# Tree attention on one core: the Q and K of 40 more heads laid side by side by GpSimd before TensorE turns them, and two groups of output rows stored in other pieces

## Chip, cores and metric

One core of a Trainium2 chip. The time is device microseconds (us) of one execution; the kernel before took 133.55 us (median of three runs, 133.35 to 133.63).

## What is computed

The reference, cut to what matters: attention over 512 tokens that are the nodes of a binary tree (parent of i is (i-1)//2), where a node sees itself and its ancestors only. There are 8 x 12 = 96 heads of dimension 64, float32 in and out.

```python
scores = np.einsum('bhqd,bhkd->bhqk', Q, K) * scale
scores = scores + (1 - mask) * (-1e9)        # mask[i, j] = 1 for j = i and its ancestors
weights = np.exp(scores - np.max(scores, axis=-1, keepdims=True))
weights = weights / (np.sum(weights, axis=-1, keepdims=True) + 1e-10)
return np.einsum('bhqk,bhkd->bhqd', weights, V).astype(np.float32)
```

## The kernel before

**Units of work.** The 96 heads go in 48 pairs. Pair i (from 8 on, the "wide" pairs) goes through these steps. *Turn* (L456 for K, L483 for Q; one call serves two pairs): TensorE transposes Q and K with an identity into the PSUM tiles `ktp` and `qtp`, and VectorE copies these to a tile `kq` (L470, L474, L478 for K, L493 for Q). *Scores* (L507, L536): TensorE adds products of mask codes and of keys with queries into PSUM, for the 128 top nodes (`s1`) and for the lower ones (`s2`); ScalarE takes the exponential (L529, L560) into bf16 tiles. *Values* (L592): 20 products per head pair of these weights with V and a column of ones, into the PSUM tile `ob`, of which there is one. *Norm* (L644): VectorE takes the reciprocal of the ones' column (L651) and multiplies (L653) into the output tile `of`.

**Loads.** Q, K and V are float32 in DRAM and become bf16 on the way: all loads but the first two are DMAs issued by GpSimd (POOL in the profile). Q and K come in blocks of 8 heads (tiles `qst`, `kst`, four of each), V in groups of 16 heads (`vst`, three). V isn't used as it lies: copies ("spreads", all on L364) bring its rows to other partitions in the `vt` tiles, of which there are two sets. VectorE makes some of these copies (a table by pair), ScalarE a few early ones, GpSimd the rest.

**Laying.** A block's Q or K can be turned in two ways. `turn_slot` (L437) transposes each head of a pair by itself: 16 transposes of 128 x 64 per call. For a block in `LAID` (8, 9, 10 and 11, so heads 64 to 95), GpSimd first copies the block into `beside["K"]` or `beside["Q"]` so that the two heads of a pair stand side by side (`lay`, L426: two copies of 128 x 512 words for a block, each for four heads), and a call has 8 transposes of 128 x 128 (L441). There is one `beside` tile for K and one for Q, so that a block can be laid only when the block laid before it has been turned.

**The order of values.** `values` does the full-width products first and the ones of half width (64 columns) last; from pair 4*LAID[0]-4 = 28 on the half-width ones stand in the middle (L630).

**GpSimd's order.** GpSimd works through a list written out by hand (`pool_program`, L676): DMA issues, spreads, lays and stores, strictly one after the other; an entry's wait holds back all behind it. DMAs are told of by eight semaphores in turn, so that a DMA also waits for the landing of the one eight before it. The outputs are stored by GpSimd too (L662), but for the last four heads, which SyncE stores at the very end. The first four heads go in four DMAs of 85, 2, 34 and 7 of the 128 partitions (`DEALT`, L669), between loads; all other stores take all partitions.

Of the kernel before, what the change touches and what calls it, by code (L numbers as in the profile page):

```python
# [119 lines left out]
def kernel(  # L120
# [7 lines left out]
    nc = tc.nc  # L128
    B, H, S, D = Q.shape
    P = nc.NUM_PARTITIONS  # L130
# [5 lines left out]
    WIDE = 8  # L136
    KB, VB, VO = 8, 16, 16
    EIGHT = 2
    LAID = (8, 9, 10, 11)
    assert NH % VB == 0  # L140

    fp32 = mybir.dt.float32
# [90 lines left out]
    issued = {(name, h) for name in ("kst", "qst") for h in (0, 1)}  # L233
# [35 lines left out]
    def head(i, a):  # L269

        return 2 * i + a if i < WIDE else 4 * (i // 2) + i % 2 + 2 * a
# [151 lines left out]
    def slots(st, i):  # L423
        return st[2 * i // KB].rearrange("p (g x) t d -> p g (x t) d", x=2)

    def lay(name, b):  # L426

        st = {"kst": ksts, "qst": qsts}[name][b]
        assert all((name, h) in issued for h in range(KB * b, KB * b + KB))
        laid[name, b] = two = beside[name[0].upper()]  # L430
        for g in range(KB // 4):
            src = st[:, 4 * g:4 * g + 4, :, :].rearrange("p (a x) t d -> p (x t) a d", x=2)
            nc.gpsimd.tensor_copy(
                out=two[:, g, :, :, :].bitcast(int32), in_=src.bitcast(int32)
            )
# [156 lines left out]
    def values(i):  # L592

        if i < NP - 1:
            obs[i] = ob = psO.tile([P, 2, 512], fp32, name="ob")
        else:
            obs[i] = ob = psS.tile([P, 2, 512], fp32, name="s1")
        e1, e2, vt = ets[i], e2s[i % NE], vts[(head(i, 0) // VB) % NV]

        vtile = VTILE if i < WIDE else WVTILE  # L600
        parts = EIGHT_PARTS if head(i, 0) >= VB * EIGHT else PARTS[i >= WIDE]
        assert all(("vt", n, head(i, a)) in issued for n in parts for a in range(2))

        def product(e, a, t, tile_v, lo=0, hi=128, **flags):
            nc.tensor.matmul(  # L605
                out=ob[lo:hi, a, 65 * t:65 * t + 65],
                lhsT=e[:, a, PLACE[t], lo:hi],
                rhs=vt[vtile[tile_v][0]][:, head(i, a) % VB, vtile[tile_v][1], 0:D + 1],
                **flags,
            )  # L610

        def firsts(a):
            for t in range(4):
                product(e1, a, t, 0, start=t == 0, stop=False)

        def halves(a, last=True):
            for t in (0, 1):
                product(e2, a, t, 1 + SELF[t], 0, 64, start=False, stop=last and t == 1)
                product(e2, a, t, 1 + t, 64, 128, start=False, stop=last and t == 1)

        def wholes(a, last=False):
            for t in (2, 3):
# [37 lines left out]
    def store(eng, h0, n, step=1, p0=0, p1=P):  # L660
        g, f = divmod(h0, VO)
        return eng.dma_start(  # L662
            out=Or[p0:p1, h0:h0 + step * (n - 1) + 1:step, :],
            in_=ofs[g][p0:p1, f:f + step * (n - 1) + 1:step, :, :].rearrange(
                "p h t d -> p h (t d)"
            ),
        )

    DEALT = (0, 85, 87, 121, P)  # L669

    def store_rows(j0, j1):

        for j in range(j0, j1):
            store(nc.gpsimd, 0, 4, 1, DEALT[j], DEALT[j + 1])

    def pool_program():  # L676

        ops = [
            (load_k, 2, 2), (load_q, 2, 2), (load_v, 0, 4), (load_v, 4, 4),
            (load_k, 4, 4), (load_q, 4, 4), (load_k, 8, 4),  # L680
            (load_q, 8, 4), (load_v, 8, 8), (load_k, 12, 4),
            (load_q, 12, 4), (load_k, 16, 8), (load_q, 16, 4), (load_rows, 1, "upper"),
            (load_rows, 1, "even"), (load_rows, 1, "odd"), (load_q, 20, 4),
            (load_k, 24, 8), (load_q, 24, 8), (load_rows, 2, "upper"),
            (load_k, 32, 8), (load_leaves, 2, 0), (load_leaves, 2, 1),
            (load_q, 32, 8), (load_rows, 3, "upper"),
            (spread_pool, (1, "Z0", 8, 16), (1, "Z1", 8, 16)),
            (load_k, 40, 8), (load_q, 40, 8), (load_leaves, 3, 0), (load_leaves, 3, 1),
            (spread_top, 2, 0, 16), (spread_pool, (2, "Z0", 0, 16), (2, "Z1", 0, 16)),
            (load_q, 48, 8), (spread_pool, (2, "X", 0, 16)),  # L690
            (load_k, 48, 8), (spread_pool, (2, "N", 0, 16)),
            (load_rows, 4, "upper"), (spread_top, 3, 0, 16),
            (load_k, 56, 8), (load_q, 56, 8), (load_leaves, 4, 0), (load_leaves, 4, 1),
            (spread_pool, (3, "X", 0, 16), (3, "N", 0, 16), (3, "Z0", 0, 16), (3, "Z1", 0, 16)),
            (load_k, 64, 8), (store_rows, 0, 2), (load_q, 64, 8), (store_rows, 2, 4),
            (load_k, 72, 8), (spread_top, 4), (store, nc.gpsimd, 4, 12), (lay, "kst", 8),
            (load_q, 72, 8), (spread_pool, (4, "X", 0, 16), (4, "N", 0, 16)),
            (lay, "qst", 8), (load_rows, 5, "upper"),
            (spread_pool, (4, "Z0", 0, 16), (4, "Z1", 0, 16)),
            (load_leaves, 5, 0), (load_leaves, 5, 1), (load_k, 80, 8), (load_q, 80, 8),  # L700
            (store, nc.gpsimd, 16, 8), (lay, "kst", 9), (load_k, 88, 8), (load_q, 88, 8),
            (lay, "qst", 9), (store, nc.gpsimd, 24, 8), (store, nc.gpsimd, 32, 16),
            (spread_top, 5), (lay, "kst", 10), (store, nc.gpsimd, 48, 16), (lay, "qst", 10),
            (spread_pool, (5, "X", 0, 16), (5, "N", 0, 16)),
            (spread_pool, (5, "Z0", 0, 16), (5, "Z1", 0, 16)),
            (lay, "kst", 11), (store, nc.gpsimd, 64, 8), (lay, "qst", 11),
            (store, nc.gpsimd, 72, 8), (spread_leaves, 5, 1),
            (store, nc.gpsimd, 80, 8), (store, nc.gpsimd, 88, 4),
        ]
        return ops  # L710
# [146 lines left out]
```

## Time and profile before

| | |
|---|---|
| median of 3 runs | 133.55 us |
| the profiled execution: its time, its span | 133.8 us, 131.9 us |
| busy in the span: PE, DVE, ACT, POOL | 114.7, 108.8, 94.4, 87.1 us |
| granted TensorE clock, mean | 0.978 |
| HBM read and written | 37.96 MB, 12.58 MB |

How to read it: PE is TensorE, DVE VectorE, ACT ScalarE, POOL GpSimd, SP SyncE. Times in the rows are us from the span's start. A row of the timeline has the start, the duration, engine, line, operation, output <- input, shape and count, and in brackets the idle time just before it with what ended it. A row of a group has the busy sum and the mean in ns. DMA share is the time of the packets as a share of 16 DMA engines; it passes 1 where packets overlap.

### The profile page before, as it was taken

Reading aid. Unit: us, or ns where it says so; the run is one execution under the profiler, and the core shown is the slowest. Engines: PE = TensorE matmul, PEld = TensorE weight load, DVE = VectorE, ACT = ScalarE, POOL = GpSimd, SP = SyncE. Lnnn points to the kernel's source line nnn. Section 1 sums busy time; section 2 is a strip of 40 time slices with the busy share of each in tenths; the row PEclk is TensorE's granted clock in tenths of the full one; section 3 lists DMA queues with packets and bytes.
Section 4 is the critical chain, followed back from the end, with each engine's and each line's share of the span. In section 5 each row is a group of like instructions: output and inputs, shape, how many; then the busy total and the mean of one; then the engine's idle time right before and its main releaser. Section 6 shows DMA issues by size and latency. Waiting matters only on the chain.

```text
span 131.9 us, 5281 instructions
## 1 busy us (share of the span) xinstructions
PE 114.7 (87%) x2286; PEld 80.4 (61%) x2289; DVE 108.8 (82%) x261; ACT 94.4 (72%) x153; POOL 87.1 (66%) x118
## 2 busy tenths in 40 slices
PE   6883999999789699899899999999988999999920
PEld 2351576676566476666577677677765766776610
DVE  3438569988999989989999999999999999877350
ACT  4358268989768957968858787787868668688900
POOL 6994624245623998799951899999999977802200
PEclk9999599999999999999999999999999999999996
DMA  3999999999999999999999999999999999999984
GB/s 122 216 190 196 198 199 205 199 199 207 206 200 205 204 202 208 209 202 205 202 208 204 244 236 305 338 204 207 203 288 285 228 391 406 400 402 402 397 315 148
DMA packets 29719, 32.28 MB, mean 245 GB/s; under 512 B 1488, under 2 KB 26704, under 8 KB 29696
## 3 DMA queue, kind: packets, MB, share of 16 engines
q0 software_dynamic: 28416, 30.68, 115.2%
q1 hardware_dynamic: 864, 0.93, 2.1%
q10 hardware_dynamic: 416, 0.33, 1.0%
q8 instruction: 18, 0.29, 0.8%
q14 instruction: 5, 0.04, 0.1%
HBM read 37.96 MB, written 12.58 MB: 383 GB/s over the span
## 4 chain that ended last, share of the span: by engine, by line
DVE 38%; PE 24%; DMA 14%; POOL 10%; issue 5%; ACT 3%; ACTq 1%; POOLq 0%
DVE of L653 12%; DVE vt L364 11%; DMA kst<-in_K_dram 8%; PE ob L605 8%; DMA qst<-in_Q_dram 6%; POOL vt L364 5%; DVE rec L651 3%; PE s L511 3%; DVE kq L493 3%; DVE kq L470 3%; DVE kq L478 3%; DVE kq L474 3%; PE s L519 2%; ACT e L560 2%; PE s L544 1%
## 5 line engine op out<-in xcount | busy, mean ns | idle before, releaser
L529 ACT ACTIVATE e<-s 128x1024 bf16<-128x1024 f32 x40 | 40.9, 1023 | 20.7 <-PE s L519 20.1
L605 PE MATMUL ob<-vt,e 128*128 128x65 bf16 (+1 forms) x940 | 39.8, 198 | 6.0 <-DVE of L653 3.0
L605 PEld LDWEIGHTS <-e 128*128 128x128 bf16 (+1 forms) x960 | 31.7, 103 | 15.9 <-DVE of L653 5.1
L560 ACT ACTIVATE e<-s 128x384 bf16<-128x384 f32 x80 | 34.7, 491 | 0.0
L653 DVE TENSOR_TENSOR of<-ob,rec 128x512 f32<-128x512 f32 x47 | 32.5, 691 | 1.6
L364 POOL COPY vt<-vst 32x512 int32<-32x512 int32 (+1 forms) x38 | 31.0, 816 | 2.9 <-PE ob L605 1.2
L364 DVE COPY vt<-vst 32x1024 bf16<-32x1024 bf16 (+6 forms) x54 | 26.8, 497 | 2.3 <-DMA vst<-in_V_dram 1.3
L662 POOL DMA_DIRECT2D out_dram<-of x13 | 12.1, 928 | 12.7 <-DVE of L653 9.2
L511 PE MATMUL s<-codes 40*128 40x512 bf16 x96 | 19.3, 398 | 0.7 <-ACT e L525 0.4
L519 PE MATMUL s<-kq 64*128 64x512 bf16 x96 | 18.5, 380 | 0.0
L651 DVE RECIPROCAL rec<-ob 128x8 f32<-128x8 f32 x47 | 9.6, 204 | 8.8 <-PE ob L605 8.0
L554 PEld LDWEIGHTS <-kq 64*128 64x128 bf16 x320 | 12.1, 94 | 4.8
L554 PE MATMUL s<-kq 64*128 64x160 bf16 (+1 forms) x320 | 14.6, 208 | 0.0
L544 PE MATMUL s<-codes 40*128 40x384 bf16 x80 | 13.6, 333 | 0.3
L493 DVE COPY kq<-qtp 128x1024 bf16<-128x1024 bf16 x20 | 13.6, 681 | 0.0
L256 POOL DMA_DIRECT2D qst<-in_Q_dram x11 | 8.3, 752 | 6.8 <-DMA vst<-in_V_dram 2.6
L525 ACT ACTIVATE e<-s 128x1024 bf16<-128x1024 f32 x8 | 8.2, 1022 | 6.0 <-PE s L519 5.9
L544 PEld LDWEIGHTS <-codes 40*128 40x128 bf16 x80 | 6.1, 94 | 7.9 <-issue 1.2
L256 POOL DMA_DIRECT2D kst<-in_K_dram x10 | 7.6, 760 | 3.9 <-PE ob L605 2.8
L470 DVE COPY kq<-ktp 128x256 bf16<-128x256 bf16 x20 | 8.3, 415 | 0.3 <-PE ktp L450 0.3
L474 DVE COPY kq<-ktp 128x256 bf16<-128x256 bf16 x20 | 8.3, 415 | 0.0
L478 DVE COPY kq<-ktp 128x512 bf16<-128x512 bf16 x20 | 8.3, 414 | 0.0
(49 smaller groups left out, 139.4 us busy)
## 6 DMA issues: line engine op xcount, KB each, us to landing
kst<-in_K_dram POOLq DMA_DIRECT2D x10, 512.0 KB, 13.2
out_dram<-of POOLq DMA_DIRECT2D x5, 1024.0 KB, 13.9
qst<-in_Q_dram POOLq DMA_DIRECT2D x9, 512.0 KB, 14.5
out_dram<-of POOLq DMA_DIRECT2D x2, 2048.0 KB, 20.8
vst<-in_V_dram POOLq DMA_DIRECT2D x12, 256.0 KB, 14.9
vst<-in_V_dram POOLq DMA_DIRECT2D x6, 512.0 KB, 14.3
out_dram<-of POOLq DMA_DIRECT2D x1, 1536.0 KB, 10.7
qst<-in_Q_dram POOLq DMA_DIRECT2D x5, 256.0 KB, 11.9
```

The source lines that it names most:

```text
L256: return nc.gpsimd.dma_start(out=kept[b][:, h0 % KB:h0 % KB + n, :, :].rearrange("p (g x) t d -> p g (x t d)", x=2), in_=wide[:, h0 // 2:( ...
L364: return copy(out=dst, in_=src)
L493: nc.vector.tensor_copy(out=qq[:, :, 0:16, :].rearrange("p b u c -> p b (u c)"), in_=halves)
L511: nc.tensor.matmul(out=sp[:, a, :], lhsT=(k1code if i < WIDE else k1wide)[64 * a:64 * a + CODE_ROWS, :], rhs=(q1code[64 * a:64 * a + CODE_ ...
L519: nc.tensor.matmul(out=sp[:, a, :], lhsT=keys(i, a, TOP), rhs=qTs[i][64 * a:64 * a + 64, :, :].rearrange("p t c -> p (t c)"), start=False, ...
L529: ) if i < WIDE else nc.scalar.activation(
L544: nc.tensor.matmul(out=flat[:, a, :, :].rearrange("p u (t c) -> p u t c", t=4)[:, :, :, 16:64], lhsT=k2wide[64 * a:64 * a + CODE_ROWS, :], ...
L554: nc.tensor.matmul(out=flat[:, a, :, lo:hi], lhsT=keys(i, a, WTILE2[t]), rhs=qT[64 * a:64 * a + 64, :, lo:hi], start=False, stop=t == 1, s ...
L560: nc.scalar.activation(out=e2s[i % NE][:, a, :, 32:128].rearrange("p t (r u) -> p t r u", u=2), in_=flat[:, a, :, :].rearrange("p u (t r) ...
L605: nc.tensor.matmul(out=ob[lo:hi, a, 65 * t:65 * t + 65], lhsT=e[:, a, PLACE[t], lo:hi], rhs=vt[vtile[tile_v][0]][:, head(i, a) % VB, vtile ...
L651: nc.vector.reciprocal(out=rec[:, a:a + n, :, :], in_=o4[:, a:a + n, :, D:D + 1])
L653: nc.vector.tensor_tensor(out=ofs[g][:, first:last + 1:step, :, :], in0=o4[:, a:a + n, :, 0:D], in1=rec[:, a:a + n, :, :].to_broadcast([P, ...
```

## The change

Three things are changed. (1) `LAID` becomes blocks 2, 3, 4, 5, 7 to 11: heads 16 to 47 and 56 to 63 are laid too, and `lay` can do one half of a block. The pair from which the order of values differs stays 28. (2) The dealt stores have three heads (0 to 2) and not four; the store after them takes heads 3 to 15. (3) Heads 32 to 34 leave the store of heads 32 to 47 and go in three DMAs of 15, 17 and 96 partitions, later in the list, among the lays of blocks 10 and 11. To make room some entries of the list change places: `spread_top` of V's group 3 goes behind the loads of heads 56 to 63.

```diff
-    LAID = (8, 9, 10, 11)
+    LAID = (2, 3, 4, 5, 7, 8, 9, 10, 11)
+    LATE = 28
...
-    def lay(name, b):
+    def lay(name, b, g0=0, g1=2):
...
-        for g in range(KB // 4):
+        for g in range(g0, g1):
...
-        elif i >= 4 * LAID[0] - 4:
+        elif i >= LATE:
...
-            store(nc.gpsimd, 0, 4, 1, DEALT[j], DEALT[j + 1])
+            store(nc.gpsimd, 0, 3, 1, DEALT[j], DEALT[j + 1])
...
-            (load_k, 24, 8), (load_q, 24, 8), (load_rows, 2, "upper"),
-            (load_k, 32, 8), (load_leaves, 2, 0), (load_leaves, 2, 1),
-            (load_q, 32, 8), (load_rows, 3, "upper"),
+            (load_k, 24, 8), (load_q, 24, 8), (load_rows, 2, "upper"), (lay, "kst", 2),
+            (load_k, 32, 8), (lay, "qst", 2, 0, 1), (load_leaves, 2, 0), (load_leaves, 2, 1),
+            (load_q, 32, 8), (lay, "qst", 2, 1, 2), (load_rows, 3, "upper"),
...
-            (lay, "qst", 9), (store, nc.gpsimd, 24, 8), (store, nc.gpsimd, 32, 16),
-            (spread_top, 5), (lay, "kst", 10), (store, nc.gpsimd, 48, 16), (lay, "qst", 10),
+            (lay, "qst", 9), (store, nc.gpsimd, 24, 8), (store, nc.gpsimd, 35, 13),
+            (spread_top, 5), (lay, "kst", 10), (store, nc.gpsimd, 32, 3, 1, 0, 15),
+            (store, nc.gpsimd, 48, 16), (lay, "qst", 10), (store, nc.gpsimd, 32, 3, 1, 15, 32),
...
-            (lay, "kst", 11), (store, nc.gpsimd, 64, 8), (lay, "qst", 11),
+            (lay, "kst", 11), (store, nc.gpsimd, 32, 3, 1, 32, P), (store, nc.gpsimd, 64, 8), (lay, "qst", 11),
```

GpSimd's rows from the loads of V's group 3 (heads 48 to 63; `vst` in the first row) to the last spread of group 2 (heads 32 to 47; `vt` 107 to 109) stand like this before the change; the load of `qst` is that of heads 48 to 55:

```order
L294 DMA vst<-in_V_dram 32x8x512 x2
L364 COPY vt_0_107<-vst 32x16x32 x4
L364 COPY vt_1_108<-vst 32x32x32 x2
L256 DMA qst<-in_Q_dram 128x4x512
L364 COPY vt_2_109<-vst 32x32x32
```

And so after it:

```order
L295 DMA vst<-in_V_dram 32x8x512 x2
L434 COPY besideK<-kst 128x512 x2
L365 COPY vt_0_107<-vst 32x16x32 x4
L365 COPY vt_1_108<-vst 32x32x32 x2
L257 DMA qst<-in_Q_dram 128x4x512
L434 COPY besideQ<-qst 128x512 x2
L365 COPY vt_2_109<-vst 32x32x32
```

Block 4's keys (heads 32 to 39) are laid ahead of six spreads, and its queries behind them and a load's issue.

TensorE's rows where it turns the queries of the first heads of block 4, behind the last products of values (`ob`, half width), before:

```order
L605 LDWEIGHTS e_1_103
L605 MATMUL ob<-vt_1_114,e_1_103 64x65
L450 LDWEIGHTS qst
L450 MATMUL qtp<-ptile,qst 64x2x64
L450 LDWEIGHTS qst
L450 MATMUL qtp<-ptile,qst 64x2x64
```

The same place after:

```order
L606 LDWEIGHTS e_1_103
L606 MATMUL ob<-vt_1_114,e_1_103 64x65
L442 LDWEIGHTS besideQ
L442 MATMUL qtp<-ptile,besideQ 128x2x64
L442 LDWEIGHTS besideQ
L442 MATMUL qtp<-ptile,besideQ 128x2x64
```

Before, 16 such transposes read the loaded tile; now 8 of double width read GpSimd's copy of it, and stand behind GpSimd's wait. TensorE's program has 4260 rows, 320 fewer than the 4580 of before; VectorE's and ScalarE's rows are the same in number and order.

More of the change, by code (lines that the diff above doesn't have):

```diff
@@ L424, in slots @@
         return st[2 * i // KB].rearrange("p (g x) t d -> p g (x t) d", x=2)
-    def lay(name, b):
+    def lay(name, b, g0=0, g1=2):
         st = {"kst": ksts, "qst": qsts}[name][b]
-        assert all((name, h) in issued for h in range(KB * b, KB * b + KB))
+        assert all((name, h) in issued for h in range(KB * b + 4 * g0, KB * b + 4 * g1))
         laid[name, b] = two = beside[name[0].upper()]
-        for g in range(KB // 4):
+        for g in range(g0, g1):
             src = st[:, 4 * g:4 * g + 4, :, :].rearrange("p (a x) t d -> p (x t) a d", x=2)
@@ L683, in pool_program @@
             (load_rows, 1, "even"), (load_rows, 1, "odd"), (load_q, 20, 4),
[L684 to L688 removed]
+            (load_k, 24, 8), (load_q, 24, 8), (load_rows, 2, "upper"), (lay, "kst", 2),
+            (load_k, 32, 8), (lay, "qst", 2, 0, 1), (load_leaves, 2, 0), (load_leaves, 2, 1),
+            (load_q, 32, 8), (lay, "qst", 2, 1, 2), (load_rows, 3, "upper"),
+            (spread_pool, (1, "Z0", 8, 16), (1, "Z1", 8, 16)), (lay, "kst", 3),
+            (load_k, 40, 8), (load_q, 40, 8), (lay, "qst", 3),
+            (load_leaves, 3, 0), (load_leaves, 3, 1), (lay, "kst", 4),
             (spread_top, 2, 0, 16), (spread_pool, (2, "Z0", 0, 16), (2, "Z1", 0, 16)),
[L690 removed]
+            (load_q, 48, 8), (lay, "qst", 4), (spread_pool, (2, "X", 0, 16)),
             (load_k, 48, 8), (spread_pool, (2, "N", 0, 16)),
[L692 to L693 removed]
+            (load_rows, 4, "upper"), (lay, "kst", 5),
+            (load_k, 56, 8), (load_q, 56, 8), (lay, "qst", 5),
+            (load_leaves, 4, 0), (load_leaves, 4, 1), (spread_top, 3, 0, 16),
             (spread_pool, (3, "X", 0, 16), (3, "N", 0, 16), (3, "Z0", 0, 16), (3, "Z1", 0, 16)),
[L695 to L696 removed]
+            (load_k, 64, 8), (store_rows, 0, 2), (load_q, 64, 8), (store_rows, 2, 3),
+            (lay, "kst", 7), (store_rows, 3, 4),
+            (load_k, 72, 8), (lay, "qst", 7), (spread_top, 4), (store, nc.gpsimd, 3, 13), (lay, "kst", 8),
             (load_q, 72, 8), (spread_pool, (4, "X", 0, 16), (4, "N", 0, 16)),
```

## Prediction

> **What bounds the kernel now.** I read the page's 40 slices first (busy tenths, 3.3 us each), then the stages, then the rows of single waits. The DMA engines are full from the second slice to the 38th, GpSimd from the 23rd to the 34th:
>
> ```profile
> POOL 6994624245623998799951899999999977802200
> DMA  3999999999999999999999999999999999999984
> ```
>
> The stages show what sets the pace (us; then busy time and count of PE, PEld, DVE, ACT, POOL; granted clock, DMA share, GB/s):
>
> ```profile
> 60.00:65.00 5.00, 4.65 (x115) 3.34 (x110) 4.82 (x12) 4.18 (x7) 4.86 (x6) 1.00 1.36 203
> 65.00:70.00 5.00, 4.66 (x112) 3.42 (x109) 4.84 (x12) 3.57 (x7) 2.80 (x4) 1.00 1.24 206
> 90.00:95.00 5.00, 4.84 (x99) 3.58 (x98) 4.84 (x12) 3.96 (x8) 5.00 (x8) 1.00 1.26 205
> ```
>
> In the middle VectorE works 4.8 of 5 us, the rest being gaps of some hundredths between instructions: the chain of pairs runs at VectorE's pace. GpSimd has room (2.80 of 5) at 65 to 70 and none at 90 to 95. The DMA queue never empties, but loads are asked for some 13 us before they land, so it doesn't hold the pairs up. What ends the program is the last pair's norm and SyncE's store behind it:
>
> ```profile
> 126.96 0.42 DVE L653 TENSOR_TENSOR of<-s,rec 128x256 f32<-128x256 f32 x1
> 127.41 0.39 SPq L662 DMA_DIRECT2D out_dram<-of  x1
> out_dram<-of POOLq DMA_DIRECT2D x1, 512.0 KB, 5.3
> out_dram<-of SPq DMA_DIRECT2D x1, 512.0 KB, 3.6
> 124.42 0.76 POOL L662 DMA_DIRECT2D out_dram<-of  x1 [3.42 <-DVE of L653]
> 127.00:128.00 1.00, 0.00 (x0) 0.00 (x0) 0.39 (x1) 0.00 (x0) 0.00 (x0) 1.00 0.57 217
> ```
>
> SyncE's store lands at 127.41 + 3.6 = 131.0, GpSimd's last at 124.42 + 5.3 = 129.7. The DMA share drops to 0.57 at 127 to 128: most DMA engines have run dry and wait for that store, while the last one still writes GpSimd's rows until 129.7. So a later norm moves the end, but for the part that hides behind the last DMA engine.
>
> **The laid transposes give TensorE nothing.** Both forms are in the trace:
>
> ```profile
> 71.68 0.79 PE L605 MATMUL ob<-vt,e 128*128 128x65 bf16 x20
> 72.30 0.61 PE L450 MATMUL qtp<-ptile,qst 128*64 128x128 bf16 x16
> 72.85 0.40 PE L511 MATMUL s<-codes 40*128 40x512 bf16 x2
> 83.04 0.89 PE L605 MATMUL ob<-vt,e 128*128 128x65 bf16 x20
> 83.77 0.61 PE L441 MATMUL ktp<-ptile,besideK 128*128 128x128 bf16 x8
> 84.31 0.40 PE L511 MATMUL s<-codes 40*128 40x512 bf16 x2
> ```
>
> Sixteen narrow transposes take 0.55 us to the next row (72.30 to 72.85), eight wide ones 0.54. Twenty calls change form, worth 20 x 0.01 = 0.2 us. Against it stands that full width follows half width at once: values take 0.62 us to the next row in the old order and 0.73 in the one that changes width twice, so up to 20 x 0.11 = 2.2 us more of TensorE. I take 0 of both, for TensorE waits for VectorE's norm there (row at 50.85 below); ends -0.2 and +2.2.
>
> **What GpSimd's 20 more copies cost VectorE.** Five blocks, Q and K, two copies each:
>
> ```profile
> L433 POOL COPY besideQ<-qst 128x512 int32<-128x512 int32 x8 | 5.3, 680 | 0.2
> L433 POOL COPY besideK<-kst 128x512 int32<-128x512 int32 x8 | 4.7, 612 | 1.1 <-PE ktp L441 0.9
> L364 POOL COPY vt<-vst 32x1024 int32<-32x1024 int32 x16 | 17.3, 1078 | 0.7
> L364 POOL COPY vt<-vst 32x512 int32<-32x512 int32 x22 | 13.8, 626 | 2.2 <-PE ob L605 1.2
> L364 DVE COPY vt<-vst 32x1024 bf16<-32x1024 bf16 x36 | 19.6, 543 | 1.9 <-DMA vst<-in_V_dram 1.3
> 70.16 0.42 DVE L364 COPY vt<-vst 32x1024 bf16<-32x1024 bf16 x1
> 99.84 1.05 DVE L364 COPY vt<-vst 32x1024 bf16<-32x1024 bf16 x1
> ```
>
> 10 x 0.68 + 10 x 0.61 = 12.9 us. VectorE's own spreads take 0.42 us when GpSimd rests (70.16) and up to 1.05 beside its work (99.84). Their mean of 0.543 makes 36 x 0.12 = 4.4 us lost to 5.3 + 4.7 + 17.3 + 13.8 = 41.1 us of GpSimd's copying, 0.11 us per us. The new 12.9 us cost 1.4 by this; 0 if none meets a spread, 12.9 x 0.11 x 2 = 2.8 if they meet twice as many.
>
> **Where TensorE will wait for GpSimd.** I add GpSimd's rows up in the new order. The load that stands ahead of the first piece waits for a landing in both kernels:
>
> ```profile
> 42.41 0.58 POOL L294 DMA_DIRECT2D vst<-in_V_dram  x1 [1.92 <-DMA kst<-in_K_dram]
> 43.03 4.86 POOL L364 COPY vt<-vst 32x512 int32<-32x512 int32 x6
> 47.84 0.76 POOL L256 DMA_DIRECT2D qst<-in_Q_dram  x1
> 48.64 1.03 POOL L364 COPY vt<-vst 32x1024 int32<-32x1024 int32 x1
> 77.44 1.20 POOL L433 COPY besideK<-kst 128x512 int32<-128x512 int32 x2
> 49.01 0.61 PE L450 MATMUL qtp<-ptile,qst 128*64 128x128 bf16 x16
> 50.85 0.79 PE L605 MATMUL ob<-vt,e 128*128 128x65 bf16 x20 [0.28 <-DVE of L653]
> ```
>
> From 43.03: block 4's keys 1.2 (44.23), six spreads 4.81 (49.04), the load's issue 0.80 (49.84), the first half of block 4's queries 0.68: 50.52. TensorE wants them at 49.01, so it waits 1.5 us; behind it stand the scores of the next pair and its values, for which VectorE's norm waits. From the turn to these values are 50.85 - 0.28 - 49.01 = 1.56 us of work, so the values start at 52.08 and not 50.85: **1.2 us**, on VectorE's path. Copies slowed before 49 us make TensorE come later to the same point, so they are covered by this wait; the ends of this term are 0 (GpSimd is earlier, or the pairs are 1.2 us late by themselves) and 1.5. Behind it the lays of blocks 5 and 7, eight copies, 5.2 us, cost 5.2 x 0.11 = **0.6 us** by the rate above. The other lays come in time by the same sum.
>
> ```profile
> 57.57 1.17 POOL L294 DMA_DIRECT2D vst<-in_V_dram  x2
> 63.37 0.77 POOL L256 DMA_DIRECT2D kst<-in_K_dram  x1
> 68.10 1.08 POOL L662 DMA_DIRECT2D out_dram<-of  x1 [1.38 <-DMA kst<-in_K_dram]
> 71.28 0.56 POOL L662 DMA_DIRECT2D out_dram<-of  x1 [2.10 <-DMA qst<-in_Q_dram]
> 72.89 0.78 POOL L256 DMA_DIRECT2D kst<-in_K_dram  x1 [1.04 <-PE ob L605]
> kst<-in_K_dram POOLq DMA_DIRECT2D x10, 512.0 KB, 13.2
> ```
>
> With `spread_top` of group 3 moved down, the load of 63.37 is issued at about 67.7. What was issued at 57.57 to 58.7 lands some 13 us later, at 71 to 72, so the queue doesn't run dry there, by 3 us. GpSimd's idle 1.38 + 2.10 + 1.04 = 4.5 us before 72.89 take the delay in but for some 1.5 us.
>
> **The stores.** Three DMAs more (15, 17 and 96 rows); bytes stay.
>
> ```profile
> out_dram<-of POOLq DMA_DIRECT2D x1, 340.0 KB, 13.8
> out_dram<-of POOLq DMA_DIRECT2D x1, 8.0 KB, 12.9
> q8 instruction: 18, 0.29, 0.8%
> ```
>
> The 8 KB store (2 rows) was issued 1.12 us behind that of 340 KB and landed 0.2 behind it: an extra small DMA costs the queue 0 to 0.2 us, three at most 0.6. GpSimd spends 0.56 to 1.08 us on issuing such a store (rows at 71.28 and 68.10), for three some 2.3. TensorE's program is fetched in 18 packets, 0.8% of 16 x 131.9 us, 0.94 us each on one DMA engine; 320 rows fewer at 0.29 MB / 4580 are 20 KB, one or two packets. I take 0 for the stores, ends -0.9 and +0.6.
>
> **The sum.** 1.2 + 0.6 = 1.8 us on the last norm. Of it 0 to 1.1 hides behind the last DMA engine (it has GpSimd's rows until 129.7; SyncE's rows flow at about 128.6 if an issue takes 1.2 us); I take 0.7. So the end moves by +1.1: 133.8 + 1.1 = 134.9 for the profiled execution, which is 0.25 over its median; for the median 133.55 + 1.1 = **134.6 us**.
>
> **Rivals.** *The queue hides it* (other side): if the pairs lose under 1.1 us, say because the wait at 49 is halved, SyncE's store still comes before the last DMA engine is free, and that engine's work decides. It has up to two fetches fewer and other dealt rows: -0.9 to +0.3, 132.7 to 133.9. For it speaks that DMA has been full for 36 slices, against it the 0.57 at the end. 34%: 21% faster, 13% the same.
>
> *GpSimd becomes the bound.* Block 8's keys are laid at 77.44 to 78.64 and turned at 83.77: 5.1 us of room. The six lays of blocks 4, 5 and 7 take 6 x 1.25 = 7.5 us out of it and give 4.5 back in the idle rows; the three issues take 2.3 more by the last lays. 5.1 - 7.5 + 4.5 - 2.3 = -0.2, and the pairs' own delay of 1.8 makes it 1.6. From there each us that GpSimd loses to VectorE, in a stretch where it never rests, goes to the end; with 3 us lost, 134.6 + 3 - 1.6 = 136.0. Against it: its copies keep nearly one pace now (means of 612 and 680 beside 0.6 at rest). 12%.
>
> *One DMA engine gets the 17 rows*: 17 x 3 KB at 400 / 16 = 25 GB/s are 2.0 us on one engine, 1.8 more than its share of a stored piece; if it is the last one, 135.3, decided at the end whatever the pairs do. In the Trainium skill, "DMA: Bandwidth & Descriptors", section "Why a DMA increments its semaphore by 16 and not by 1", the number of engines is the largest up to 16 that divides the outer size, so 17 rows go to one; it also names an exception with rows spread evenly. No view here tells the engines apart. 6%.
>
> **How the numbers follow.** My forecast (+0.3 to +1.9) has 48%. Range 133.0 to 136.3: down into the hidden case, up to the wait at its bound with all contention (1.5 + 1.4 + 0.3 for TensorE's changes of width, less 0.5). Faster by over 0.2% (about what a measurement of this kernel can tell from no change) 0.22, within 0.14, slower 0.64.
>
> **What would show it.** TensorE idle 1 us or more before the turn at 49 to 51, ended by GpSimd's `besideQ`; the values at L605 starting near 52.1; the mean of VectorE's 32x1024 spreads over 0.543; SyncE's store issued near 129.2. Wrong, if that store is issued before 128.5, if TensorE's turns get shorter than 0.54, or if the DMA share falls under 1 in the middle.

## The result, and the profile after

The changed kernel takes 138.07 us (median of 6 runs, 137.2 to 140.34) against 133.52 us (6 runs, 133.08 to 133.63) on the same chip: a ratio of 1.0326, 95% interval 1.0288 to 1.0364, so **4.5 us slower**. (The run of 140.34 was a slow one and is left out of the ratio, which therefore lies a little under that of the medians.) The forecast was slower too, but by 1.1 us, and the time lies outside its range. The profiled execution took 138.32 us with a span of 136.5 us, against 133.8 and 131.9.

From here on the lines of the kernel after are one higher than before: the lay is L434, the turn of a laid block L442, the values L606, the norm L654, the store L663, the spreads L365, the loads of Q and K L257. In the runs further down the same statements stand on other lines where lines were added.

**The wait that was forecast.** TensorE's rows of the kernel after, where the queries of block 4 are turned:

```profile
50.76 0.62 PE L442 MATMUL qtp<-ptile,besideQ 128*128 128x128 bf16 x8 [1.31 <-POOL besideQ L434]
52.23 0.79 PE L606 MATMUL ob<-vt,e 128*128 128x65 bf16 x20
```

And GpSimd's ahead of them:

```profile
44.53 4.80 POOL L365 COPY vt<-vst 32x512 int32<-32x512 int32 x6
49.29 0.76 POOL L257 DMA_DIRECT2D qst<-in_Q_dram  x1
50.09 1.16 POOL L434 COPY besideQ<-qst 128x512 int32<-128x512 int32 x2
```

The turn waits 1.31 us for the first half of the lay (50.09 plus about 0.6), and the values start at 52.23; the forecast had 50.52, 1.5 and 52.08. VectorE's spreads are slower as forecast as well; the group in the kernel after:

```profile
L365 DVE COPY vt<-vst 32x1024 bf16<-32x1024 bf16 x36 | 20.9, 581 | 1.7 <-DMA vst<-in_V_dram 1.1
```

581 ns in place of 543, so 36 x 0.038 = 1.4 us: just what was worked out for all 20 copies, of which the sum then counted 0.6.

**The wait that was not.** GpSimd's rows of the kernel after, 30 us later:

```profile
79.42 0.61 POOL L434 COPY besideK<-kst 128x512 int32<-128x512 int32 x1
82.73 0.61 POOL L434 COPY besideK<-kst 128x512 int32<-128x512 int32 x1 [2.70 <-PE ktp L442]
83.29 0.78 POOL L257 DMA_DIRECT2D qst<-in_Q_dram  x1
92.10 0.77 POOL L257 DMA_DIRECT2D kst<-in_K_dram  x1
```

What it waits for, in TensorE's rows of the same kernel:

```profile
82.05 0.62 PE L442 MATMUL ktp<-ptile,besideK 128*128 128x128 bf16 x8
```

The two loads behind it, in the kernel before:

```profile
78.59 0.76 POOL L256 DMA_DIRECT2D qst<-in_Q_dram  x1
87.12 0.77 POOL L256 DMA_DIRECT2D kst<-in_K_dram  x1
```

The second half of laying the keys of block 8 stands idle for 2.70 us, because the one `besideK` tile still holds the second half of block 7, which TensorE turns at 82.05. Before, block 8 was the first block laid, and the tile held nothing that TensorE still had to turn. Behind the waiting copy, in GpSimd's strict order, stands the load of `qst` for heads 72 to 79: issued at 83.29 and not at 78.59, 4.7 us late. The wait is 2.7 of them; the other 2.0 are GpSimd's own added work, for the lay begins at 79.42, where before it began at 77.44. All loads behind it are as late: K of heads 80 to 87 goes out at 92.10, and not at 87.12. What this does to the DMA queue is seen in the windows (us; busy time and count of PE, PEld, DVE, ACT, POOL; granted clock, DMA share, GB/s), before:

```profile
84.00:86.00 2.00, 2.00 (x42) 1.39 (x40) 1.95 (x7) 1.37 (x4) 1.96 (x3) 1.00 1.14 283
88.00:90.00 2.00, 2.00 (x42) 1.50 (x38) 1.93 (x6) 1.59 (x4) 1.96 (x3) 1.00 1.40 199
80.00:100.00 20.00, 19.36 (x383) 14.22 (x379) 19.38 (x45) 15.46 (x26) 19.54 (x27) 1.00 1.21 263
```

And after:

```profile
84.00:86.00 2.00, 1.79 (x33) 1.24 (x30) 1.92 (x4) 1.59 (x4) 1.92 (x3) 1.00 0.76 181
88.00:90.00 2.00, 2.00 (x44) 1.51 (x42) 1.96 (x6) 1.56 (x3) 1.92 (x3) 1.00 0.56 69
80.00:100.00 20.00, 18.86 (x355) 13.67 (x354) 19.26 (x43) 14.93 (x27) 17.02 (x23) 1.00 1.08 205
```

The queue runs dry (shares of 0.76 and 0.56), and from 80 to 100 us it moves 20 x (263 - 205) = 1160 KB less. At the 378 GB/s at which it moves stores at the end (row below), that is 3.1 us; at the 199 GB/s of the row of 88 to 90 us before, 5.8, so it is an estimate. The forecast named a DMA share under 1 in the middle as a sign against it.

**The end.** The kernel after:

```profile
127.63 0.76 POOL L663 DMA_DIRECT2D out_dram<-of  x1 [3.41 <-DVE of L654]
130.62 0.39 SPq L663 DMA_DIRECT2D out_dram<-of  x1
out_dram<-of POOLq DMA_DIRECT2D x1, 512.0 KB, 6.7
out_dram<-of SPq DMA_DIRECT2D x1, 512.0 KB, 5.0
132.00:133.00 1.00, 0.00 (x0) 0.00 (x0) 0.00 (x0) 0.00 (x0) 0.00 (x0) 0.79 1.02 378
```

SyncE's store is issued 130.62 - 127.41 = 3.2 us later (the pairs' delay: it follows the last pair's norm) and takes 5.0 us to land in place of 3.6, since the DMA engines are still full at 132 to 133, where before they ran dry at 127. It lands at 135.6 in place of 131.0: +4.6. So two things are late at the end, the pairs and the queue. With an empty queue (some 2.8 us to landing, as in runs below) the pairs alone would make +2.4, already more than the forecast's 1.1. The time from issue to landing of this last store is the gauge that the runs below are read by: near 3, the queue stood waiting for the store; at 5 or more, the store waited in the queue.

### The profile page after: what moved, and what is told of

It reads as the page before. It is cut to its first block, busy times and chain, and to the rows that moved or that the text cites. A ratio compares the mean times of both kernels' runs of the same rounds, so it can differ in the third digit from the quotient of the medians.

```text
span 136.5 us, 4981 instructions
## 1 busy us (share of the span) xinstructions
PE 116.2 (85%) x2126; PEld 81.5 (60%) x2129; DVE 111.2 (81%) x261; ACT 94.4 (69%) x153; POOL 101.9 (75%) x141
## 4 chain that ended last, share of the span: by engine, by line
DVE 37%; DMA 20%; PE 18%; POOL 11%; issue 7%; ACT 1%; ACTq 1%; POOLq 0%
DVE of L654 12%; DMA vst<-in_V_dram 12%; DVE vt L365 9%; DMA qst<-in_Q_dram 9%; PE ob L606 7%; DVE rec L652 4%; DVE kq L494 4%; POOL vt L365 3%; DVE kq L471 3%; DVE kq L479 3%; DVE kq L475 3%; PE s L512 2%; POOL kst L245 2%; PE qtp L442 2%; POOL vst L245 2%
## 5 line engine op out<-in xcount | busy, mean ns | idle before, releaser
L606 PE MATMUL ob<-vt,e 128*128 128x65 bf16 (+1 forms) x940 | 39.8, 198 | 6.9 <-DVE of L654 3.8
L606 PEld LDWEIGHTS <-e 128*128 128x128 bf16 (+1 forms) x960 | 31.7, 103 | 16.7 <-DVE of L654 5.6
L654 DVE TENSOR_TENSOR of<-ob,rec 128x512 f32<-128x512 f32 x47 | 32.5, 692 | 1.6
L365 POOL COPY vt<-vst 32x512 int32<-32x512 int32 (+1 forms) x38 | 31.2, 821 | 1.7
L365 DVE COPY vt<-vst 32x1024 bf16<-32x1024 bf16 (+6 forms) x54 | 29.0, 536 | 2.0 <-DMA vst<-in_V_dram 1.1
L663 POOL DMA_DIRECT2D out_dram<-of x16 | 14.5, 911 | 6.0 <-DVE of L654 6.0
L434 POOL COPY besideK<-kst 128x512 int32<-128x512 int32 x18 | 11.3, 654 | 3.1 <-PE ktp L442 2.7
L257 POOL DMA_DIRECT2D qst<-in_Q_dram x11 | 8.3, 752 | 5.6 <-DMA vst<-in_V_dram 2.7
L442 PE MATMUL qtp<-ptile,besideQ 128*128 128x128 bf16 x144 | 11.1, 219 | 1.3 <-POOL besideQ L434 1.3
L434 POOL COPY besideQ<-qst 128x512 int32<-128x512 int32 x18 | 11.2, 653 | 0.2
L442 PE MATMUL ktp<-ptile,besideK 128*128 128x128 bf16 x144 | 11.1, 219 | 0.3 <-DVE kq L479 0.3
```

The costliest lines, as they stand in the source:

```text
L365: return copy(out=dst, in_=src)
L434: nc.gpsimd.tensor_copy(out=two[:, g, :, :, :].bitcast(int32), in_=src.bitcast(int32))
L442: nc.tensor.transpose(out=out(dst), in_=two[:, 2 * i % KB // 4, s, :, :].rearrange("p a d -> p (a d)"), identity=ptile[:, 0:128],)
L606: nc.tensor.matmul(out=ob[lo:hi, a, 65 * t:65 * t + 65], lhsT=e[:, a, PLACE[t], lo:hi], rhs=vt[vtile[tile_v][0]][:, head(i, a) % VB, vtile ...
L654: nc.vector.tensor_tensor(out=ofs[g][:, first:last + 1:step, :, :], in0=o4[:, a:a + n, :, 0:D], in1=rec[:, a:a + n, :, :].to_broadcast([P, ...
```

## Experiments

Theory 1 after the result: GpSimd's wait for the shared tile holds the loads back, the DMA queue runs dry, and nothing gives that back. Its rivals: the pairs' own delay (the wait at 50 us, slower spreads) sets the end; the stores cost it; TensorE loses by the changes of width. All ratios are against the kernel before on the same chip, whose medians were 133.47 to 133.65 us. Where a tile more was needed, the output tiles are five instead of six; two runs with five show that this costs nothing by itself (0.9991 and 1.0006).

**The parts alone.** First the stores: the kernel before with the new pieces of heads 0 to 2 and 32 to 34, and no more lays.

```diff
-            store(nc.gpsimd, 0, 4, 1, DEALT[j], DEALT[j + 1])
+            store(nc.gpsimd, 0, 3, 1, DEALT[j], DEALT[j + 1])
...
+            (spread_top, 5), (lay, "kst", 10), (store, nc.gpsimd, 32, 3, 1, 0, 15),
```

> The kernel before with the new pieces of the stores alone (heads 0 to 2 dealt, heads 32 to 34 as 15, 17 and 96 rows behind 35 to 47), no block laid beyond the four of before. Theory 1 (the loss of 4.5 us is the DMA queue running dry at 84 to 95 us, because GpSimd waits 2.7 us in the middle of laying block 8's keys for TensorE to turn block 7, whose copy lies in the same tile): nothing of that is in here, 133.2 to 134.1. Theory 2 (the pairs' delay on VectorE and TensorE, 3.2 us at the last norm, is the loss): 133.2 to 134.1 too. Theory 3 (the stores' new pieces cost, by three DMAs more and one DMA engine with 17 rows): 134.5 to 138.

Measured: 134.12 us, ratio 1.0037 (1.0004 to 1.0071). The stores cost 0.5 us, near the upper end (0.6) that the prediction gave them.

Then the lays alone: the kernel after with the stores of before.

```diff
-            store(nc.gpsimd, 0, 3, 1, DEALT[j], DEALT[j + 1])
+            store(nc.gpsimd, 0, 4, 1, DEALT[j], DEALT[j + 1])
...
-            (spread_top, 5), (lay, "kst", 10), (store, nc.gpsimd, 32, 3, 1, 0, 15),
+            (spread_top, 5), (lay, "kst", 10), (store, nc.gpsimd, 48, 16), (lay, "qst", 10),
```

> The change without its stores: five blocks more are laid, the stores are those of before. Theories 1 and 2: 137.4 to 138.4, as the whole change. Theory 3: under 137, by what the stores cost.

Measured: 137.44 us, 1.0301 (1.0251 to 1.0351). The lays make nearly all of it, and the same wait of 2.7 us stands in the profile.

Then TensorE's side of the lays without GpSimd's: the kernel before, in which the turns of blocks 2 to 5 and 7 take the wide form and read a tile of zeros. This leaves Q and K of these heads out of the result.

```diff
-    qsts, ksts, vsts, laid = {}, {}, {}, {}
+    qsts, ksts, vsts = {}, {}, {}
+    laid = {(name, b): ghost for name in ("kst", "qst") for b in (2, 3, 4, 5, 7)}
```

> The kernel before with the wide transposes for blocks 2 to 5 and 7, but with no copy by GpSimd: they read one tile of zeros, so that the scores of these blocks leave Q and K out (five output tiles for six). It prices TensorE's new form. By the rows of the trace: 133.2 to 134.2. If the changes of width cost their 2.2 us: 134.8 to 135.8. If the wide form helps TensorE: under 133.0.

Measured: 133.51 us, 0.9991 (0.9973 to 1.0008). The form gains nothing, and the 2.2 us that changes of width might have cost aren't there. The prediction's 0 stands.

Then GpSimd's side without TensorE's: the copies of these blocks go to a tile that nobody reads, at the places where the change has them; TensorE turns these blocks in the narrow form, and the stores are those of before.

```diff
-    LAID = (2, 3, 4, 5, 7, 8, 9, 10, 11)
+    LAID = (8, 9, 10, 11)
...
-        laid[name, b] = two = beside[name[0].upper()]
+        two = ghost
+        if b in LAID:
+            laid[name, b] = two = beside[name[0].upper()]
```

> The lays of the change without its stores, but blocks 2 to 5 and 7 are copied into a tile that nobody reads, and TensorE turns them as before (five output tiles for six). GpSimd does all its new work and nobody waits for it, nor it for a turn. Theory 1 (the loss is GpSimd's wait for the turn of block 7, which lets the DMA queue run dry): most of the 3.9 us of the lays alone goes, 134.2 to 135.4. Rival (the 20 copies themselves, by GpSimd's time and by slowing VectorE): 136.5 to 137.6, as the lays alone.

Measured: 134.88 us, 1.0117 (1.0041 to 1.0192). So the copies as such cost 1.2 us, with an interval of 0.5 to 2.6. The other 137.44 - 134.88 = 2.6 us go with laying into the shared tiles, that is with the waits between GpSimd and TensorE, both ways; the turns' form, the third part, cost nothing. The parting isn't clean: in this run the values still wait twice for GpSimd, 1.2 us in all.

**The hold.** The lay of block 8's keys moved behind the load that it held:

```diff
-            (load_k, 72, 8), (lay, "qst", 7), (spread_top, 4), (store, nc.gpsimd, 3, 13), (lay, "kst", 8),
+            (load_k, 72, 8), (lay, "qst", 7), (spread_top, 4), (store, nc.gpsimd, 3, 13),
             (load_q, 72, 8), (spread_pool, (4, "X", 0, 16), (4, "N", 0, 16)),
+            (lay, "kst", 8),
```

> The change with one entry moved: block 8's keys are laid behind the load of heads 72 to 79 and two spreads, so that GpSimd's wait for TensorE's turn of block 7 holds back no load. Theory 1: the stretch of 84 to 95 us keeps its DMA share near 1.2, the last norm stays 2 to 3.2 us late, SyncE's store lands about 2.7 to 3.6 us behind it: 135.0 to 136.3. Theory 2: the last norm sets the end in the change already, 137.2 to 138.2.

Measured: 137.12 us, 1.0224 (1.0162 to 1.0287). The wait is gone but for 0.2 us, yet only 1 us comes back (1.4 by the ratios): 0.8 above theory 1's bounds and just under the rival's. The profiled execution had a mean clock of 0.954, and its pairs were already 2.1 us late at the norm of pair 12 (in the kernel after 0.2), so its rows tell little; K of heads 80 to 87 still went out at 90.35, 3.2 us late. Taken alone it speaks for neither.

The same with one half of that lay, the half that waited:

```diff
-            (load_k, 72, 8), (lay, "qst", 7), (spread_top, 4), (store, nc.gpsimd, 3, 13), (lay, "kst", 8),
+            (load_k, 72, 8), (lay, "qst", 7), (spread_top, 4), (store, nc.gpsimd, 3, 13), (lay, "kst", 8, 0, 1),
             (load_q, 72, 8), (spread_pool, (4, "X", 0, 16), (4, "N", 0, 16)),
+            (lay, "kst", 8, 1, 2),
```

> The changed kernel with one edit: the second half of laying the keys of heads 64 to 71, which waited 2.71 us for the shared tile, stands behind the load of Q of heads 72 to 79 and the two spreads instead of ahead of them. Theory 1 (that wait holds the loads and leaves the DMA queue dry) expects 135.0 to 136.2 us, with the load issued near 80 us. The rival (the pairs' own lateness sets the end in any case) expects 137 to 138 us.

Measured: 136.56 us, 1.0224 (1.0166 to 1.0281), 0.4 above theory 1's bounds and under the rival's. GpSimd's rows and a wait of this run show why no more came back:

```profile
79.41 0.78 POOL L257 DMA_DIRECT2D qst<-in_Q_dram  x1
90.03 0.78 POOL L257 DMA_DIRECT2D kst<-in_K_dram  x1
POOL besideQ L434 <- PE qtp L442: 1.4, 1, 1.4
```

The first load is 0.8 us late now and not 4.7, but the next lay waits for the other shared tile, 1.4 us, and the load behind it is 2.9 us late again.

Two tiles for each of K and Q, used in turn, so that no lay waits for the one before:

```diff
+        besides[name] = [
+            beside[name], consts.tile([P, KB // 4, 8, 2, D], bf16, name=f"beside{name}2")
+        ]
...
-        laid[name, b] = two = beside[name[0].upper()]
+        if g0 == 0:
+            laid[name, b] = besides[name[0].upper()][dealt[name] % 2]
+            dealt[name] += 1
+        two = laid[name, b]
```

> The change with two tiles to lay into for K and two for Q, in turn (and five output tiles for six, to make room, which the trace of the change says are free long before), so that no lay waits for the turn of the block before it. Theory 1: 134.8 to 136.3, as with the moved lay or better. Theory 2: 137.2 to 138.2.

Measured: 135.34 us, 1.0133 (1.0108 to 1.0157). One more tile for each takes back 138.07 - 135.34 = 2.7 us. The last store of this run:

```profile
129.40 0.39 SPq L670 DMA_DIRECT2D out_dram<-of  x1
out_dram<-of SPq DMA_DIRECT2D x1, 512.0 KB, 2.8
```

2.8 us to its landing: by the gauge the queue stands waiting for the store, and what is left is the pairs' delay (129.40 - 127.41 = 2.0 us).

With that, the lay of block 4's queries moved ahead of four spreads, which takes the wait at 50 us away too:

```diff
-            (spread_top, 2, 0, 16), (spread_pool, (2, "Z0", 0, 16), (2, "Z1", 0, 16)),
-            (load_q, 48, 8), (lay, "qst", 4), (spread_pool, (2, "X", 0, 16)),
+            (spread_top, 2, 0, 16), (lay, "qst", 4), (spread_pool, (2, "Z0", 0, 16), (2, "Z1", 0, 16)),
+            (load_q, 48, 8), (spread_pool, (2, "X", 0, 16)),
```

> Two tiles each to lay into, and block 4's queries are laid ahead of two spreads and a load's issue and not behind them, so that TensorE shouldn't wait 1.3 us for them at 49 to 51. If the pairs' delay sets what is left of the loss (1.7 us at two tiles): 133.9 to 134.8. If DMA or GpSimd's lateness sets it: 135.0 to 135.6.

Measured: 135.82 us, 1.0162 (1.0144 to 1.0179). This is 0.2 above the second bound. From the norm of pair 8 to that of pair 14 this run takes 0.1 us less than the kernel before, where the run with two tiles alone takes 1.7 more, so the long wait is gone (three of at most 0.5 us are left); but nothing is gained. The lay, put ahead, now waits 0.8 us itself for its block to land, K of heads 80 to 87 goes out at 89.12 and not at 88.22, and 239 GB/s pass from 80 to 100 us in place of 257. The last store is issued 0.6 us earlier (128.81) and takes 4.2 us to land in place of 2.8: what the pairs got, the queue lost.

The kernel after without the lays of block 7, so that the tile is free when block 8 comes:

```diff
-    LAID = (2, 3, 4, 5, 7, 8, 9, 10, 11)
+    LAID = (2, 3, 4, 5, 8, 9, 10, 11)
```

> The change without laying block 7 (heads 56 to 63): two lays fewer, and block 8's lay finds its tile free. Theory 1: 134.8 to 136.0, as with two tiles. Rival (loss by the copies' number): a fifth of the lays' loss goes, 136.8 to 137.5.

Measured: 137.18 us, 1.0283 (1.0236 to 1.0329), which theory 1 had not foreseen. Rows of the run:

```profile
51.17 0.66 PE L442 MATMUL qtp<-ptile,besideQ 128*128 128x128 bf16 x8 [1.96 <-POOL besideQ L434]
75.84 2.65 POOL L365 COPY vt<-vst 32x512 int32<-32x512 int32 x4 [2.55 <-PE ob L606]
82.71 1.29 DVE L365 COPY vt<-vst 32x1024 bf16<-32x1024 bf16 x1
85.97 1.20 DVE L365 COPY vt<-vst 32x1024 bf16<-32x1024 bf16 x1
89.20 0.77 POOL L257 DMA_DIRECT2D kst<-in_K_dram  x1
94.29 0.61 POOL L434 COPY besideK<-kst 128x512 int32<-128x512 int32 x1 [1.96 <-PE ktp L442]
132.88 0.39 SPq L663 DMA_DIRECT2D out_dram<-of  x1
out_dram<-of SPq DMA_DIRECT2D x1, 512.0 KB, 2.8
```

The profiled execution was the slowest of the four, 138.46 us. The load is half mended (89.20), but here the pairs are 5.5 us late at the end, and the store lands 2.8 us behind its issue: the pairs set this end. TensorE waits 1.96 us for the lay at 50 us, and two spreads of VectorE that met GpSimd's take 1.29 and 1.20 us in place of 0.42; these rows make at most 1.96 + 0.87 + 0.78 = 3.6 of the 5.5 us. The rest is not settled. GpSimd is rid of one wait and has got two others: 2.55 us for TensorE's values ahead of four spreads, and 1.96 us for `besideK` once more, now in the middle of block 9. So this run doesn't test the wait alone; but the pairs set its end, and that they can be so late with block 8's wait gone is more than theory 1 says.

**The queue by itself.** Is it the late load, or the copies and lays around it? The kernel before with seven copies of a loaded block into a tile that nobody reads, ahead of the load:

```diff
+    def spare(b, n):
+        for g in range(n):
+            src = ksts[b][:, 0:4, :, :].rearrange("p (a x) t d -> p (x t) a d", x=2)
+            nc.gpsimd.tensor_copy(
+                out=ghost[:, g % 2, :, :, :].bitcast(int32), in_=src.bitcast(int32)
+            )
...
-            (load_q, 72, 8), (spread_pool, (4, "X", 0, 16), (4, "N", 0, 16)),
+            (spare, 6, 7), (load_q, 72, 8), (spread_pool, (4, "X", 0, 16), (4, "N", 0, 16)),
```

> The kernel before, with seven more GpSimd copies of a loaded block into a tile that nobody reads (7 x 0.61 = 4.3 us), put directly ahead of the load of Q of heads 72 to 79 in GpSimd's order, so that this load and all behind it are issued some 4 us later; no lay, no store piece and no order of TensorE's is changed, except that the output tiles are five. Theory 1 (the transfers have no slack there: a load issued 4 us late leaves the DMA queue dry for part of that, and nothing gives it back) expects 135.5 to 137.5 us with a DMA share below 1.6 in a stretch near 84 to 90 us. The rival (the queue's stock of issued transfers covers it, and the pairs alone set the end) expects at most 134.2 us.

Measured: 137.05 us, 1.0257 (1.0226 to 1.0289). Windows, GpSimd's loads and the end of this run:

```profile
80.00:100.00 20.00, 16.46 (x318) 11.81 (x312) 16.85 (x38) 12.72 (x23) 19.68 (x27) 1.00 1.10 206
83.05 0.76 POOL L258 DMA_DIRECT2D qst<-in_Q_dram  x1
91.43 0.77 POOL L258 DMA_DIRECT2D kst<-in_K_dram  x1
128.21 0.39 SPq L671 DMA_DIRECT2D out_dram<-of  x1
out_dram<-of SPq DMA_DIRECT2D x1, 512.0 KB, 6.6
```

The load goes out 4.5 us late (in the changed kernel 4.7), and with it all that stands behind it in GpSimd's order; as little passes (206 and 205 GB/s), and 3.5 us are lost, with no lay added and no store changed. The pairs are only 0.8 us late; the last store waits in the queue, 6.6 us.

The same seven copies where GpSimd idles:

```diff
-            (load_k, 64, 8), (store_rows, 0, 2), (load_q, 64, 8), (store_rows, 2, 4),
+            (load_k, 64, 8), (store_rows, 0, 2), (load_q, 64, 8), (spare, 6, 2), (store_rows, 2, 3),
+            (spare, 6, 3), (store_rows, 3, 4), (spare, 6, 2),
```

> The same seven copies as in the run that holds the load, but put among the dealt stores where GpSimd stands idle at 66 to 73 us, so that no load is issued later. If it is the held load that costs, this one gives 133.3 to 134.3 us (0.5 us of contention with VectorE at most); if the copies themselves cost it, the same as the run that holds the load.

Measured: 133.76 us, 1.0006 (0.9989 to 1.0023). The spreads and the windows of this run:

```profile
L366 DVE COPY vt<-vst 32x1024 bf16<-32x1024 bf16 x36 | 21.0, 582 | 1.5 <-DMA vst<-in_V_dram 0.8
80.00:100.00 20.00, 19.33 (x383) 14.31 (x380) 19.37 (x45) 15.56 (x27) 19.54 (x27) 1.00 1.21 265
```

The same copies, the same slowing of VectorE's spreads as in the changed kernel (582 ns), and nothing lost: no load is late (K of heads 80 to 87 at 87.05). These two runs settle that a late load costs, and not the copies. That it is the main loss of the change too rests on the same lateness and the same 205 GB/s there, and on the 2.7 us that two tiles took back.

Three copies in place of seven ahead of the load:

```diff
-            (spare, 6, 7), (load_q, 72, 8),
+            (spare, 6, 3), (load_q, 72, 8),
```

> The run that holds the load, with three copies ahead of it instead of seven (3 x 0.61 = 1.8 us). If the queue had the 3 us of slack on which the forecast counted, nothing is lost: 133.4 to 133.8 us, and as much moved from 80 to 100 us as before (263 GB/s). If the slack is about 1 us, which seven copies with 4.4 us of lateness and 3.5 us of loss suggest, 0.5 to 1.1 us are lost: 134.0 to 134.7 us, and 245 to 258 GB/s.

Measured: 135.16 us, 1.0127 (1.01 to 1.0154), more than either theory of the slack had.

```profile
80.52 0.76 POOL L258 DMA_DIRECT2D qst<-in_Q_dram  x1
125.93 0.39 SPq L671 DMA_DIRECT2D out_dram<-of  x1
out_dram<-of SPq DMA_DIRECT2D x1, 512.0 KB, 6.1
```

1.9 us of lateness cost 1.7 us: the queue has no slack worth the name. That it runs dry is not seen here: in windows of 2 us from 80 to 100 the share never falls under 1 (lowest 1.03), only fewer bytes pass, 241 GB/s in place of 263. In this execution the pairs even end 1.5 us earlier than before (125.93 against 127.41), and the store waits 6.1 us all the same. Why they are early is open: TensorE's clock was 1.00 in place of 0.91 from 2 to 20 us, but it was 1.00 in the run with the copies in idle time too, whose store goes out at 127.36. So the pairs' delay, read from one execution of each kernel, is good to about 1 us.

**The lays of before.** Since copies and waits only cost: the kernel before with no lays at all. The lays' entries leave GpSimd's list, and every pair's values stand in the order of the early pairs.

```diff
-    LAID = (8, 9, 10, 11)
+    LAID = ()
...
-        elif i >= 4 * LAID[0] - 4:
+        elif i >= NP:
```

> The kernel before with no block laid at all: the copies and wide turns of heads 64 to 95 are taken out too, and every pair's values stand as the early pairs' do. The wide turns alone gained TensorE nothing (0.9991), so theory 1 (a lay gives nothing and its copies cost VectorE about 0.1 us per us beside them, 1.2 us for 18 copies) expects 0.5 to 1 us less at the pairs for these 16 copies of 9.9 us, and 132.6 to 133.6 us in all, since the transfers may hold the end. The rival, that the lays of before pay at the end because TensorE's last blocks turn in fewer instructions, expects 134 us or more.

Measured: 135.16 us, 1.0103 (1.0071 to 1.0135): theory 1 missed; the lays of before and the order of values that goes with them do pay, 1.4 us by the ratio. (The profiled execution took 135.35 us, but its span, 132.3, is only 0.4 longer than that of the kernel before, so its rows show but a part of this.) TensorE's rows of this run behind 112 us that have an idle time marked "issue":

```profile
112.41 0.33 PE L450 MATMUL ktp<-ptile,kst 128*64 128x128 bf16 x5 [1.28 <-issue]
118.89 0.50 PE L605 MATMUL ob<-vt,e 128*128 128x65 bf16 x11 [0.64 <-issue]
125.91 0.19 PE L605 MATMUL ob<-vt,e 128*64 128x65 bf16 x1 [0.49 <-issue]
```

"issue" is idle time in which the engine waited for nothing that the profile shows. Its rows add up to 3.7 us behind 10 us of this run (three more stand between 87 and 100), and to 0.2 us in the kernel before.

Only the lays of heads 80 to 95 kept, with the order of values of before:

```diff
-    LAID = (8, 9, 10, 11)
+    LAID = (10, 11)
...
-        elif i >= 4 * LAID[0] - 4:
+        elif i >= 28:
```

> The kernel before with the lays of heads 64 to 79 taken out and those of heads 80 to 95 kept; the order of the values stays as before. In the run without any lay the pairs ran early up to pair 40 and fell behind only at the last four pairs, so theory 1 (a lay pays only where TensorE has nothing else to put beside its turns, at the end) expects the end as before or a little earlier, 133.0 to 133.7 us, with the last norm 0 to 0.6 us earlier. The rival (each of the four lays gives a like share of the 1.6 us) expects 134.2 to 134.5 us.

Measured: 133.80 us, 1.0025 (1.0002 to 1.0047). That lies between the two bounds, just above theory 1's: most of the loss is back. This run gave back two things, the lays of the last two blocks and the order of values from pair 28 on; which of them pays is not told apart. One long gap of TensorE is left, and GpSimd has one of the same kind that ends at the same time:

```profile
88.62 0.76 POOL L256 DMA_DIRECT2D kst<-in_K_dram  x1 [1.27 <-issue]
88.78 0.64 PE L450 MATMUL ktp<-ptile,kst 128*64 128x128 bf16 x16 [1.21 <-issue]
```

No run beat the kernel before by more than its interval. Theory 1's bounds held, within 0.1 us, for the two parts alone, the two tiles, the copies alone and the two runs with seven copies; they were too low for the lay behind the load, the half lay and the run without block 7, in each of which the pairs were 2.4 to 5.5 us late.

**Side by side**: when K of heads 80 to 87 went out, what passed from 80 to 100 us, and the last store.

| kernel | median us | K 80 issued | GB/s | SyncE's store issued, to landing |
|---|---|---|---|---|
| before | 133.5 | 87.12 | 263 | 127.41, 3.6 |
| form alone | 133.51 | 86.45 | 266 | 126.28, 4.4 |
| seven copies in idle time | 133.76 | 87.05 | 265 | 127.36, 3.5 |
| stores alone | 134.12 | 88.08 | 265 | 126.59, 4.8 |
| two tiles | 135.34 | 88.22 | 257 | 129.40, 2.8 |
| three copies ahead of the load | 135.16 | 89.16 | 241 | 125.93, 6.1 |
| two tiles, queries laid earlier | 135.82 | 89.12 | 239 | 128.81, 4.2 |
| copies alone | 134.88 | 89.21 | 236 | 129.52, 3.0 |
| without block 7 | 137.18 | 89.20 | 240 | 132.88, 2.8 |
| half a lay later | 136.56 | 90.03 | 226 | 129.77, 3.9 |
| lay behind the load | 137.12 | 90.35 | 224 | 130.04, 4.6 |
| seven copies ahead of the load | 137.05 | 91.43 | 206 | 128.21, 6.6 |
| lays alone | 137.44 | 91.74 | 204 | 129.93, 4.6 |
| after | 138.07 | 92.10 | 205 | 130.62, 5.0 |

The last three columns are of one execution each. Read by the last one there are two kinds of end: with 2.8 to 3.0 the pairs set it, with 4.2 and more the queue does. In between, as in the kernel before (3.6), both are nearly level: with the form alone the pairs end 1.1 us earlier than before, and the time is the same.

## Why the prediction was wrong, point by point

- *The laid transposes give TensorE nothing*: right for the blocks of this change (0.9991); the changes of width cost nothing either.
- *The wait at 49 us, 1.2 us*: right where it falls. The turn waited 1.31 us, the values started at 52.23 (forecast 52.08), and the norm of pair 14 came 1.2 us late. That it reaches the end whole is not shown: with two tiles, taking it away moved the last store by only 0.6 us (129.40 to 128.81).
- *Slower spreads, 1.4 us in all*: right in size (36 x 0.038 us). But 0.6 was counted, on the ground that what falls before 49 us is covered. The pairs ended 3.2 us late and not 1.8. The two terms at full size, 1.2 and 1.4, would make 2.6, but that they add up was not tried: the copies alone, with no wait for a lay, end 2.1 us late.
- *What hides behind the last DMA engine, 0.7 us*: wrong, and so is the rival in which the queue hides the delay. The queue was not done sooner but later, and SyncE's store took 1.4 us more to land. (The 1.2 us of an issue from which 0 to 1.1 was worked out stands in no row.)
- *The stores, 0*: 0.5 us, within the ends given.
- **The step that failed** is that the loads behind GpSimd's new lays were taken to go out in time, or late for nothing. The prediction says "The other lays come in time by the same sum", and that GpSimd's idle time takes the delay in "but for some 1.5 us", which then has no price. The sum asked whether GpSimd's copy is ready when TensorE wants it, and that held: TensorE waited for one lay only. It didn't ask whether the shared tile is free when GpSimd wants to write it. That wait is 2.70 us at 80 us; with 2.0 us of GpSimd's own added work it makes the load of 78.59 4.7 us late, and GpSimd's strict order passes it on to every later load. The run that makes this load as late, with no lay added, loses 3.5 us. "The queue doesn't run dry there, by 3 us" held at the place it speaks of (a share of 1.24 from 70 to 74 us in the kernel after), and wasn't asked again for the loads behind. So most of the 4.5 us is the load's lateness; the stores and the pairs' delay make up the rest with it, and they can't simply be added, as the two kinds of end show.
- *Loads are asked for 13 us before they land*: true (13.2), but not a stock of 13 us of work: 1.9 us of lateness cost 1.7 us. What stands in the queue goes at 199 GB/s while loads pass (88 to 90 us, before) but at 378 when only stores do (132 to 133, after), so the store of 12 heads ahead of this load is gone sooner than its bytes suggest; that this is where the slack went is inferred, not tried.
- *Rivals*: that GpSimd becomes the bound, at 136.0 us with 12%, named the right engine and very nearly the place (block 8's keys), but priced its work, not its wait, and let the price reach the end through the pairs and not through the loads. That one DMA engine gets the 17 rows is not told apart by any view. In the Trainium skill, "SBUF — State Buffer", section "SBUF: two separate sides", it says that the port pair which GpSimd shares with VectorE's operations in a 2-port mode is an exclusive lock: whichever starts first has it for the whole instruction, and the other fully blocks. Whether these copies run in such a mode is seen in no view, but the rows agree in kind: a spread of 0.42 us takes up to 1.29 beside GpSimd's copies, no longer than itself and one such copy (1.1 us) together; and by the pair of seven copies that slowing, in one place, cost nothing and, in the other, wasn't what cost.

## What to carry to other kernels

Where one engine issues the loads in strict order, price every instruction that is put ahead of a load by its own waits too: for what it writes, and not only for who waits for what it wrote. A copy into a single shared buffer ties two engines both ways, and a second buffer took back 2.7 of 4.5 us here. With DMA engines that are full from end to end, as here, a late load can cost nearly its whole lateness (1.7 of 1.9 us, 3.5 of 4.5), although the loads were asked for some 13 us before they landed; and the time from issue to landing of the last store is a quick sign of whether the queue or the compute sets the end.

## What the runs showed of the hardware

- 160 fewer, wider transposes in the middle of TensorE's stream gained nothing (0.9991). The run without any lay has 128 more transposes late in the program and another order of values from pair 28 on; in it TensorE stands idle in gaps of 0.34 to 1.28 us for nothing that the profile shows, 3.7 us in all, 0.2 before. Which of the two brings the gaps, and how, was not tried; with two blocks laid, GpSimd idles 1.27 us in the same way at the same time as TensorE, so the cause need not lie in TensorE. The packets of the DMA queue for instructions don't tell: they are 18 in this run and 18 before.
- A load that was issued some 7 us ahead of its first data (78.59 to about 86 us, an estimate: the windows before fall from 283 GB/s at 84 to 86 us to 199 at 88 to 90, the pace of loads) still had no slack: 1.9 us of delay cost 1.7, 4.5 cost 3.5.
